# Moving the weight sums of the seven-product tiles from VectorE to GpSimd, and starting the first feed-forward with four ordinary tiles in place of five

## The chip, the core and the metric

The kernel runs on one core of a Trainium2 chip, in one launch. The metric is the device time of that launch in microseconds (us), lower is better. Four things matter on the core here: TensorE (PE in the profile: matmuls, results in PSUM), VectorE (DVE), ScalarE (ACT) and GpSimd (POOL), each with a queue of its own that runs in order, and the SP queue, which issues the loads of weights.

## What is computed

One hybrid decoder layer in float32, 512 tokens, width 1024: a SwiGLU feed-forward of width 2816, then a mixer (three groups of dilated attention with four heads each beside a gated linear recurrence, merged by sigmoid gates), then a second feed-forward; each has a norm before and after it. Cut to what matters here:

```python
def swiglu(x, w_gate, w_up, w_down):
    return (jax.nn.silu(x @ w_gate) * (x @ w_up)) @ w_down

f = swiglu(rms_norm(h, ffn1_norm_pre), ffn1_w_gate, ffn1_w_up, ffn1_w_down)
h = h + 0.5 * rms_norm(f, ffn1_norm_post)
proj = rms_norm(h, mix_norm_pre) @ w_in      # q, k, v, recurrence, gates
...
h = h + rms_norm(merged @ w_out, mix_norm_post)
f = swiglu(rms_norm(h, ffn2_norm_pre), ffn2_w_gate, ffn2_w_up, ffn2_w_down)
h = h + 0.5 * rms_norm(f, ffn2_norm_post)
```

## The kernel before

**Split numbers.** Each float32 operand of a matmul is held as two parts, hi and lo, and a product is three matmuls (hi times hi, hi times lo, lo times hi). The function `split` makes the parts: ScalarE copies the source to hi (L269), VectorE subtracts hi from the source to get lo (L270). Both operands of that subtraction lie in SBUF.

**The stream of weights.** `raw_of` loads the weights in the order in which they are used, mostly 128x2048 values at a time, from the SP queue (L215) into a tile called `raw`, of which there are two. The split parts go into `w8` tiles (four) and `w4` tiles (two). A new load waits until a `raw` tile has been read to the end, and a new split waits until TensorE has used the `w8` tile that it overwrites.

**Two kinds of tiles.** A feed-forward has 22 column tiles f of 128 columns, each with a gate and an up product. An *ordinary* tile makes both with `gemm` (L282 to L284): 2 x 8 x 3 = 48 matmuls of 512 columns. A *seven-product* tile (`seven`, L594 to L596) makes the same two results with seven products of half the size, p1 to p7: 7 x 4 x 3 = 84 matmuls of 256 columns. It needs sums of the four weight blocks u0, u1, g0, g1 and sums of blocks of the activations:

- `w_forms` makes the weight forms. Four additions of 128x512 (L570, L571, L572, L575, all VectorE) give u0+u1, u0+u1+g0 (both in the tile `s12`), u0+g0 (in place in `raw`), and u0+u1+g0+g1 (in place in `raw`). Four splits follow: a (for p1 and p2, straight from `raw`), b (from `s12`, for p6 and p5), c (from `raw`, for p7 and p4) and d (for p3). The last addition overwrites g1, so it comes after split a has read it.
- `x_forms` makes the activation forms for the first feed-forward, in five steps: `scaled`, then `first` (p1, p2, and t1), `second` (t2, p5, p7), `third` (p6, p3), `fourth` (p4). The steps need the norm's factor, so they come behind the first ordinary tile, one step behind each ordinary tile.
- The tiles t1, t2 and `s12` share two buffers (tag "s"): the first `s12` can only be written once split p5 has read t1.

**The order of the first feed-forward** (`ffn_order`, NSTD[1] = 5): ordinary tiles f = 0 to 4, then `prep` of tile 5 (its `w_forms`), then the first half of the down product of part 0 (f = 0 to 3, 48 matmuls, L388 to L390), then seven-product tiles 5 to 21, each with the `prep` of the next ahead of it and half a down product behind some of them. The second feed-forward begins with three ordinary tiles. The mixer has 16 seven-product tiles more: twelve pairs of query and key columns and four pairs of gate columns. That makes 17 + 16 + 19 = 52.

**What sets the order on an engine.** A scheduler orders each engine's instructions when the program is built, by priority and by estimated times; `high_priority` pulls weight splits (AHEAD) and reads of PSUM (EVAC) forward. On the chip each engine follows that order without exception, so an instruction that waits holds up everything behind it on its engine.

Of the kernel before, what the change touches and what calls it, by code (L numbers as in the profile page):

```python
# [19 lines left out]
KC = D // P  # L20
NF = 22
FF_PARTS = ((0, 4), (4, 8), (8, 12), (12, 16), (16, 22))
NSTD = {1: 5, 2: 3}
NG = 3
NH = 4
EPS = 1e-6
# [22 lines left out]
def ffn_order(n):  # L49

    order = [("std", f) for f in range(NSTD[n])]
    early = NSTD[n] >= FF_PARTS[0][1]
    order.append(("prep", NSTD[n]))
    if early:
        order.append(("down", 0, 0))
    for a, (f0, f1) in enumerate(FF_PARTS):
        fs = range(max(f0, NSTD[n]), f1)
        halves = () if a == 0 else (1,) if a == 1 and early else (0, 1)  # L60
        for i, f in enumerate(fs):
            if f + 1 < NF:
                order.append(("prep", f + 1))
            c, k = len(fs), len(halves)
            order.append(("prod", f, a - 1, halves[i * k // c:(i + 1) * k // c]))
    return order


def part_blocks(a):

    return (FF_PARTS[a][1] - FF_PARTS[a][0]) // 2
# [85 lines left out]
def hybrid_layer(ctx: ExitStack, tc: tile.TileContext, xT: bass.AP, xN: bass.AP, wst: bass.AP,  # L157
                 first: bass.AP, rows: bass.AP, consts: bass.AP, bias: bass.AP, out: bass.AP):
    nc = tc.nc
    DVE, ACT, PE = nc.vector, nc.scalar, nc.tensor  # L160

    cpool = ctx.enter_context(tc.tile_pool(name="cpool", bufs=1))
    bpool = ctx.enter_context(tc.tile_pool(name="bpool", bufs=6))
# [25 lines left out]
    def fb(b, sl=slice(0, D)):  # L189
        return facc[:, 2 * b:2 * b + 2, :].rearrange("p k t -> p (k t)")[:, sl]  # L190
# [16 lines left out]
    def raw_of(key):  # L207

        g, i = state["g"], state["i"]
        grp = groups[g]  # L210
        if i == 0:
            w = grp[-1][1] + grp[-1][2]
            raw = wpool.tile([P, RAW_W], F32, name="raw", tag="raw", bufs=2)
            src = bass.AP(tensor=wst.tensor, offset=wst.offset + state["off"], ap=[[w, P], [1, w]])
            nc.sync.dma_start(raw[:, :w], src)  # L215
            state["raw"] = raw
            state["off"] += w * P
        k, o, w = grp[i]
        assert k == key, (k, key)
        src = state["raw"][:, o:o + w]  # L220
        if i + 1 == len(grp):
            state["g"], state["i"] = g + 1, 0
        else:
            state["i"] = i + 1
        return src

    def fetch(key, slot=None, ahead=0):

        with tc.high_priority(offset=ahead if slot else state["ahead"]):
            src = raw_of(key)  # L230
            w = src.shape[-1]
            t = slot() if slot else w8() if w > 512 else w4()
            split(t[:, 0, :w], t[:, 1, :w], src)
            return t[:, 0, :w], t[:, 1, :w]

    def w8():
        return wpool.tile([P, 2, 1024], F32R, name="w8", tag="w8", bufs=4)

    def w4():
        return wpool.tile([P, 2, 512], F32R, name="w4", tag="w4", bufs=2)  # L240
# [27 lines left out]
    def split(dh, dl, src):  # L268
        ACT.activation(dh, src, AF.Copy)  # L269
        DVE.tensor_sub(dl, src, dh.bitcast(F32))  # L270

    def acc_ps():
        return psum.tile([P, T], F32, name="acc", tag="acc", bufs=5)

    def aux_ps():
        return psum.tile([P, T], F32, name="aux", tag="aux", bufs=3)

    def tmp(name):
        return tpool.tile([P, T], F32, name=name, tag="t")
# [104 lines left out]
    def tokens(ps, ws, x, b, fill=lambda: None):  # L384
        bl = slice(b * P, (b + 1) * P)
        for k in range(x.n):
            wh, wl = (w.rearrange("p (k c) -> p k c", k=2)[:, k % 2, :] for w in ws[k // 2])
            PE.matmul(ps, x.hi[k][:, bl], wh, start=k == 0, stop=False)  # L388
            PE.matmul(ps, x.hi[k][:, bl], wl, start=False, stop=False)  # L389
            PE.matmul(ps, x.lo[k][:, bl], wh, start=False, stop=k == x.n - 1)  # L390
            if k == x.n // 2 - 1:
                fill()
# [171 lines left out]
    def w_forms(key):  # L564

        with tc.high_priority(offset=AHEAD):
            raw = raw_of(key)
            u0, u1, g0, g1 = (raw[:, i * 512:(i + 1) * 512] for i in range(4))
            s12 = spool[0].tile([P, 2, 512], F32, name="s12", tag="s", bufs=2)
            DVE.tensor_add(s12[:, 1, :], u0, u1)  # L570
            DVE.tensor_add(s12[:, 0, :], s12[:, 1, :], g0)  # L571
            DVE.tensor_add(u0, u0, g0)  # L572
            a, b, c, d = w8(), w8(), w8(), w4()
            split(a[:, 0, :], a[:, 1, :], raw[:, 1024:2048])
            DVE.tensor_add(g1, s12[:, 0, :], g1)  # L575
            split(b[:, 0, :], b[:, 1, :], s12.rearrange("p s c -> p (s c)"))
            split(c[:, 0, :], c[:, 1, :], raw[:, 0:1024])
            split(d[:, 0, :], d[:, 1, :], g1)
            lo, hi = slice(0, 512), slice(512, 1024)
            return {"p1": a[:, :, lo], "p2": a[:, :, hi], "p6": b[:, :, lo], "p5": b[:, :, hi],  # L580
                    "p7": c[:, :, lo], "p4": c[:, :, hi], "p3": d}
# [42 lines left out]
    def ffn(n, x, r, forms_x, apool, pss):  # L624
        t, steps = forms_x
        acts = {}

        def act_at(f):

            if f // 4 not in acts:  # L630
                at = apool.tile([P, 8, T], F32R, name="act", tag="act", bufs=3)
                acts[f // 4] = Act([at[:, j, :] for j in range(4)], [at[:, 4 + j, :] for j in range(4)])
            return acts[f // 4].hi[f % 4], acts[f // 4].lo[f % 4]

        def part(a):
            f0, f1 = FF_PARTS[a]
            his, los = zip(*(act_at(f) for f in range(f0, f1)))
            return Act(his, los)

        def std_out(psg, psu, f):  # L640

            g, u = tmp("g"), tmp("u")
            if r is None:
                ACT.activation(g, psg, AF.Silu)
                DVE.tensor_mul(u, psu, g)
            else:
                DVE.tensor_mul(g, psg, r)
                ACT.activation(g, g, AF.Silu)
                DVE.tensor_mul(u, psu, r)
                DVE.tensor_mul(u, u, g)  # L650
            split(*act_at(f), u)

        def wd():
            return apool.tile([P, 2, 1024], F32R, name="wd", tag="wd", bufs=2)

        def down(a, half):
            ws = [fetch(("down", n, a, half, kk), wd, AHEAD) for kk in range(part_blocks(a))]
            for b in range(4):
                ps, y = acc_ps(), fb(b, FHALVES[half])
                tokens(ps, ws, part(a), b)  # L660
                if a == 0:
                    ACT.activation(y, ps, AF.Copy)
                else:
                    DVE.tensor_add(y, ps, y)

        def prod(f, w, a, hs_):
            g, u = tmp("g"), tmp("u")
            seven(t, w, aux_ps()[:, :HB], [g[:, h] for h in HALVES], [u[:, h] for h in HALVES])
            for half in hs_:
                down(a, half)  # L670
            ACT.activation(g, g, AF.Silu)
            DVE.scalar_tensor_tensor(u, g, -1.0, u, op0=ALU.mult, op1=ALU.mult)
            split(*act_at(f), u)

        keys = [(w, n, i) for i in range(NSTD[n]) for w in ("gate", "up")]
        forms = {}
        for ev in ffn_order(n):
            if ev[0] == "std":
                j = ev[1]
                while len(pss) < 2 * j + 2:  # L680
                    pss.append(acc_ps())
                    gemm(pss[-1], fetch(keys[len(pss) - 1]), x)
                std_out(pss[2 * j], pss[2 * j + 1], j)
                if j < len(steps):
                    steps[j]()
            elif ev[0] == "prep":
                forms[ev[1]] = w_forms(("gu", n, ev[1]))
            elif ev[0] == "down":
                down(ev[1], ev[2])
            else:  # L690
                prod(ev[1], forms.pop(ev[1]), ev[2], ev[3])
        a = len(FF_PARTS) - 1
        return lambda half, kk: ("down", n, a, half, kk), part_blocks(a), part(a)
# [28 lines left out]
    u1 = act_two(ap1)  # L722
# [20 lines left out]


    end1 = ffn(1, u1, r1, x_forms("g1a", r1, ap1), ap1, pss)
    new_h()
    for b in range(4):
# [16 lines left out]
    with ExitStack() as mx:  # L764
# [53 lines left out]
        t, steps = forms_of(um, um_t[:2], um_t[2:], apool, False)  # L818
# [171 lines left out]
    with ExitStack() as mx:  # L990
# [144 lines left out]
        for c in range(KC):  # L1135
# [16 lines left out]
                 {(1, 3): lambda: (bd2.turn(0), bd2.turn(1))})  # L1152
    keys = [(w, 2, i) for i in range(NSTD[2]) for w in ("gate", "up")]
    pss = gemm_first(keys[:NFIRST], u2, [spare(ap2)[2]],
# [127 lines left out]
```

## Time and profile before

| what | value |
|---|---|
| device time, median of 3 runs | 1244.78 us (1244.69 to 1245.48) |
| profiled execution, its own time | 1245.37 us |
| its span from the first to the last instruction | 1243.6 us |
| granted TensorE clock over the span | 0.998 |
| VectorE additions in `w_forms` | 4 x 52 |
| GpSimd instructions | 51 |

The profile is of one execution. Its time of 1245.37 us is 1.8 us more than its span (launch and end lie outside the span) and 0.6 us above the median of the three runs. A row such as `start us, us, engine line op out<-in xcount` gives when a run of equal instructions started, how long it took and which program line it comes from; a matmul's shown duration overlaps the next one's, so the pace of TensorE is read from the distance between starts.

### The profile page before, as it was taken

To read this page: it belongs to the slowest core of one execution; us is meant where nothing else is said; L and a number is where in the kernel's file an instruction comes from. 1 tells how busy PE (TensorE), PEld (TensorE's weight loads), DVE (VectorE), ACT (ScalarE), POOL (GpSimd) and SP (SyncE) were. 2 spreads that over 40 slices of the span, in tenths; PEclk is the share of its full clock that TensorE was granted. 3 is DMA by queue.
4 is the path that set the end of the run, shared out by engine and by line. 5 is a ranking of instruction groups with operands and counts; after the bars stand their busy time and mean duration, and the time that the engine had idled before them with its cause. 6 is when DMAs were issued, how large, how long until landed. Compare 5 with 4: busy or idle time off the path is not lost.

```text
span 1243.6 us, 19076 instructions
## 1 busy us (share of the span) xinstructions
PE 1232.1 (99%) x7748; PEld 1117.6 (90%) x7748; DVE 930.4 (75%) x1473; ACT 664.3 (53%) x1100; POOL 26.2 (2%) x51
## 2 busy tenths in 40 slices
PE   9999999999999999999999999999999999999997
PEld 8899999999878899999988887888899999999986
DVE  7996777796576588888575898864798667777755
ACT  7555444455355365666544788734565544445432
POOL 0000000000002000000000000000100000000000
PEclk9999999999999999999999999999999999999999
DMA  6222222235424223222243222224443222222241
GB/s 242 102 79 103 101 102 102 101 126 184 167 90 144 85 95 103 77 89 91 100 172 102 70 99 102 102 102 169 142 130 136 103 103 102 103 103 73 103 182 67
DMA packets 27383, 141.37 MB, mean 114 GB/s; under 512 B 2976, under 2 KB 6176, under 8 KB 13216
## 3 DMA queue, kind: packets, MB, share of 16 engines
q1 hardware_dynamic: 20016, 122.86, 27.9%
q0 software_dynamic: 7280, 17.30, 4.1%
q8 instruction: 60, 0.98, 0.3%
q14 instruction: 27, 0.22, 0.1%
HBM read 129.67 MB, written 6.29 MB: 109 GB/s over the span
## 4 chain that ended last, share of the span: by engine, by line
PE 89%; DVE 6%; ACT 4%; issue 1%; DVEq 0%; ACTq 0%
PE acc L594 11%; PE acc L595 11%; PE acc L596 11%; PE acc L388 7%; PE acc L389 7%; PE acc L390 7%; PE acc L282 6%; PE acc L283 6%; PE acc L284 6%; PE aux L595 3%; PE aux L594 3%; PE aux L596 3%; PE acc L793 1%; PE acc L795 1%; PE acc L794 1%
## 5 line engine op out<-in xcount | busy, mean ns | idle before, releaser
L270 DVE TENSOR_TENSOR w<-raw,w 128x1024 fp32r<-128x1024 f32 (+1 forms) x241 | 257.9, 1074 | 97.2 <-ACT w L269 64.7
L269 ACT ACTIVATE w<-raw 128x1024 fp32r<-128x1024 f32 (+1 forms) x241 | 225.2, 938 | 181.3 <-DVE raw L575 61.0
L594 PE MATMUL acc<-big,w 128*128 128x256 f32 x896 | 255.4, 285 | 0.0
L595 PE MATMUL acc<-big,w 128*128 128x256 f32 x896 | 254.4, 284 | 0.0
L596 PE MATMUL acc<-big,w 128*128 128x256 f32 x896 | 254.1, 284 | 0.0
L594 PEld LDWEIGHTS acc<-big,w 128*128 128x128 f32 x896 | 171.6, 192 | 1.0
L595 PEld LDWEIGHTS acc<-big,w 128*128 128x128 f32 x896 | 171.7, 192 | 0.6
L596 PEld LDWEIGHTS acc<-big,w 128*128 128x128 f32 x896 | 171.7, 192 | 0.0
L601 ACT ACTIVATE c<-acc 128x256 f32<-128x256 f32 x172 | 65.2, 379 | 81.4 <-PE acc L596 78.1
L389 PE MATMUL acc<-wd,act 128*128 128x512 f32 x256 | 99.8, 390 | 0.0
L388 PE MATMUL acc<-wd,act 128*128 128x512 f32 x256 | 99.6, 390 | 0.0
L390 PE MATMUL acc<-wd,act 128*128 128x512 f32 x256 | 99.4, 389 | 0.0
L594 PE MATMUL aux<-big,w 128*128 128x256 f32 x288 | 81.5, 283 | 0.0
L595 PE MATMUL aux<-big,w 128*128 128x256 f32 x288 | 81.5, 283 | 0.0
L596 PE MATMUL aux<-big,w 128*128 128x256 f32 x288 | 81.4, 283 | 0.0
L594 PE MATMUL acc<-tx,w 128*128 128x256 f32 x272 | 77.2, 284 | 0.0
L596 PE MATMUL acc<-tx,w 128*128 128x256 f32 x272 | 77.0, 283 | 0.0
L595 PE MATMUL acc<-tx,w 128*128 128x256 f32 x272 | 77.0, 283 | 0.0
L282 PE MATMUL acc<-big,w 128*128 128x512 f32 x192 | 74.7, 389 | 0.0
L283 PE MATMUL acc<-big,w 128*128 128x512 f32 x192 | 74.7, 389 | 0.0
L284 PE MATMUL acc<-big,w 128*128 128x512 f32 x192 | 74.7, 389 | 0.0
L270 DVE TENSOR_TENSOR w<-s,w 128x1024 fp32r<-128x1024 f32 x52 | 63.7, 1224 | 10.2 <-ACT w L269 10.1
(316 smaller groups left out, 2753.0 us busy)
## 6 DMA issues: line engine op xcount, KB each, us to landing
raw<-in_w SPq DMA_DIRECT2D x110, 1024.0 KB, 4.8
big<-act POOLq DMA_DIRECT2D x6, 512.0 KB, 3.4
gains<-in_rows POOLq DMA_DIRECT2D x5, 512.0 KB, 5.0
h<-in_x SPq DMA_DIRECT2D x8, 256.0 KB, 5.0
h<-in_xn POOLq DMA_DIRECT2D x4, 512.0 KB, 7.6
kept_m<-h POOLq DMA_DIRECT2D x4, 512.0 KB, 2.9
h<-kept_m POOLq DMA_DIRECT2D x4, 512.0 KB, 5.4
kept<-h POOLq DMA_DIRECT2D x4, 512.0 KB, 3.4
```

Source lines behind the costliest of these rows:

```text
L269: ACT.activation(dh, src, AF.Copy)
L270: DVE.tensor_sub(dl, src, dh.bitcast(F32))
L282: PE.matmul(ps, wh, xh, start=first, stop=False)
L283: PE.matmul(ps, wh, xl, start=False, stop=False)
L284: PE.matmul(ps, wl, xh, start=False, stop=last)
L388: PE.matmul(ps, x.hi[k][:, bl], wh, start=k == 0, stop=False)
L389: PE.matmul(ps, x.hi[k][:, bl], wl, start=False, stop=False)
L390: PE.matmul(ps, x.lo[k][:, bl], wh, start=False, stop=k == x.n - 1)
L594: PE.matmul(ps, wh, xh, start=start and k == 0, stop=False, skip_group_check=True)
L595: PE.matmul(ps, wh, xl, start=False, stop=False, skip_group_check=True)
L596: PE.matmul(ps, wl, xh, start=False, stop=k == 3, skip_group_check=True)
L601: ACT.activation(c, ps, AF.Copy)
```

## The change

Two edits. All four additions in `w_forms` go to GpSimd, in every seven-product tile. And the first feed-forward starts with four ordinary tiles (f = 0 to 3), so that tile 4 becomes a seven-product tile; behind the last ordinary tile all steps of `x_forms` that are left are issued (`third` and `fourth` together).

```diff
-NSTD = {1: 5, 2: 3}
+NSTD = {1: 4, 2: 3}
...
-    DVE, ACT, PE = nc.vector, nc.scalar, nc.tensor
+    DVE, ACT, PE, POOL = nc.vector, nc.scalar, nc.tensor, nc.gpsimd
...
             s12 = spool[0].tile([P, 2, 512], F32, name="s12", tag="s", bufs=2)
-            DVE.tensor_add(s12[:, 1, :], u0, u1)
-            DVE.tensor_add(s12[:, 0, :], s12[:, 1, :], g0)
-            DVE.tensor_add(u0, u0, g0)
+            POOL.tensor_add(s12[:, 1, :], u0, u1)
+            POOL.tensor_add(s12[:, 0, :], s12[:, 1, :], g0)
+            POOL.tensor_add(u0, u0, g0)
             a, b, c, d = w8(), w8(), w8(), w4()
             split(a[:, 0, :], a[:, 1, :], raw[:, 1024:2048])
-            DVE.tensor_add(g1, s12[:, 0, :], g1)
+            POOL.tensor_add(g1, s12[:, 0, :], g1)
...
                 std_out(pss[2 * j], pss[2 * j + 1], j)
-                if j < len(steps):
-                    steps[j]()
+                for step in steps[j:] if j == NSTD[n] - 1 else steps[j:j + 1]:
+                    step()
```

The weights of tile 4 are then streamed as one 128x2048 block (up and gate side by side), which the host's packing follows by itself.

## The prediction

> **What bounds the kernel now.** I read first the page, then the stretches of 31.09 us, then the groups by line, then the timelines around the first seven-product tile.
>
> ```profile
> span 1243.6 us, 19076 instructions
> PE 1232.1 (99%) x7748; PEld 1117.6 (90%) x7748; DVE 930.4 (75%) x1473; ACT 664.3 (53%) x1100; POOL 26.2 (2%) x51
> ...
> PE 89%; DVE 6%; ACT 4%; issue 1%; DVEq 0%; ACTq 0%
> ```
>
> TensorE is busy in 1232.1 of 1243.6 us and carries 89% of the chain that ended last. VectorE, which is relieved, carries 6%.
>
> ```profile
> 0.00:31.09 31.09, 30.04 (x132) 25.58 (x133) 23.73 (x46) 22.98 (x44) 0.20 (x4) 1.00 0.68 242
> 31.09:62.18 31.09, 31.09 (x139) 25.75 (x138) 30.94 (x38) 18.28 (x22) 0.00 (x0) 1.00 0.29 102
> ...
> 155.45:186.54 31.09, 31.09 (x218) 29.17 (x217) 23.41 (x35) 14.22 (x22) 0.00 (x0) 1.00 0.29 102
> ...
> 497.44:528.53 31.09, 31.00 (x263) 30.82 (x262) 27.10 (x56) 19.84 (x49) 0.00 (x0) 1.00 0.23 77
> ...
> 746.16:777.25 31.09, 29.70 (x130) 24.05 (x129) 24.98 (x33) 25.26 (x34) 0.00 (x0) 1.00 0.30 102
> ...
> 901.61:932.70 31.09, 31.09 (x240) 30.13 (x239) 30.33 (x38) 20.58 (x29) 1.49 (x2) 1.00 0.42 130
> ```
>
> The columns are the length, then busy time and instructions of TensorE, its weight loads, VectorE, ScalarE and GpSimd. Where TensorE idles (30.04 at the start, 29.70 in the recurrence) no weight sum is made. Where sums are made it stands still for 0 to 0.09 us in 31.09. VectorE is full in two stretches, 30.94 us in the second and 30.33 us where the second feed-forward starts: TensorE does not wait for it there, but little is in reserve.
>
> ```profile
> L594 PE MATMUL acc<-big,w 128*128 128x256 f32 x896 | 255.4, 285 | 0.0
> ...
> L282 PE MATMUL acc<-big,w 128*128 128x512 f32 x192 | 74.7, 389 | 0.0
> ```
>
> The last column, idle time ahead of the group, is zero for both kinds of matmul: TensorE runs at its own pace.
>
> **The tile that changes its kind.** The pace, from starts:
>
> ```profile
> 61.22 0.39 PE L388 MATMUL acc<-wd,act 128*128 128x512 f32 x1
> ...
> 72.10 0.28 PE L594 MATMUL acc<-big,w 128*128 128x256 f32 x1
> ...
> 82.17 0.28 PE L594 MATMUL acc<-big,w 128*128 128x256 f32 x1
> ```
>
> Between 61.22 and 72.10 lie the 48 matmuls of half a down product: 10.88 us, 0.227 each. Between 72.10 and 82.17 lie the 84 of one seven-product tile: 10.07 us, 0.120 each. Tile 4 loses 48 of the first kind and gains 84 of the second: **-0.8 us**. That is all the second edit can bring.
>
> **The additions that leave VectorE.**
>
> ```profile
> L570 DVE TENSOR_TENSOR s<-raw x52: 681/686/691, 51.4 to 1158.7; 128x512 f32<-128x512 f32 x52
> ...
> 39.82 0.68 DVE L650 TENSOR_TENSOR u<-u,g 128x512 f32<-128x512 f32 x1
> 40.42 1.22 DVE L270 TENSOR_TENSOR big<-h,big 128x1024 fp32r<-128x1024 f32 x1
> 41.55 0.68 DVE L270 TENSOR_TENSOR act<-u,act 128x512 fp32r<-128x512 f32 x1
> 42.15 1.22 DVE L480 TENSOR_TENSOR t<-h 128x1024 f32<-128x1024 f32 x1
> 43.29 2.35 DVE L270 TENSOR_TENSOR w<-raw,w 128x1024 fp32r<-128x1024 f32 x2
> ```
>
> One addition lasts 0.686 us; from start to start a 128x512 operation takes 0.60 us (39.82 to 40.42) and a 128x1024 one 1.13 us (40.42 to 41.55). So 208 additions free 208 x 0.60 = 125 us of VectorE. I cost that at **0**: the engine that sets the end does not wait for VectorE where the sums are made. At the most it is the few hundredths of a microsecond per stretch shown above, under 0.5 us in all.
>
> **What one addition takes on GpSimd.** No row shows a GpSimd addition. The ends are 0.68 us (the same operation on VectorE) and 1.22 us (VectorE on 128x1024: as many elements as GpSimd must read if it takes its two operands one after the other). I take 1.22: the only GpSimd rows here are short memsets and DMA issues, nothing that shows it at VectorE's rate. [...]
>
> **Where the path tightens: the first seven-product tile.** Tile 4 now begins one ordinary tile earlier, when VectorE is full. In the built order of the changed kernel VectorE does this from 43.29 on: both splits of the down weights and split a of tile 4 (3 x 1.13), two PSUM reads (1.20), t2 (1.13), a product (0.60), split p5 (1.13): 7.5 us, until 50.8. Only then is the buffer of t1 free, and GpSimd can begin. From there to the lo part of tile 3's result stand seven VectorE operations of 1.13 and five of 0.60, **10.9 us, all with two operands in SBUF**, and two PSUM reads (1.20). Among them are splits b, c, d of tile 4 and d of tile 5, behind all **eight** GpSimd additions of the two tiles. None can be passed: ScalarE's split b is queued ahead of its c and d splits, its Silu and tile 3's hi part, and everything on VectorE stands in line behind split b.
>
> TensorE: its ordinary tiles end at 61.22 - 10.88 = 50.34. Then come 36 down matmuls of f = 0 to 2 (8.16), 24 of p5 and p1 (2.88), 9 of p6 (1.08), and at 62.5 the 12 down matmuls that need tile 3's lo part. Before, that part had an ordinary tile's time more.
>
> When is it ready? The price depends on whether a GpSimd addition and a VectorE operation that both read two SBUF operands go on side by side.
>
> - **Taking turns**: 50.8 + 10.9 + 8 x 1.22 = 71.5; TensorE waits 9.0 us (with 0.68 per addition: 67.1, 4.6 us).
> - **Side by side**:
>
> ```profile
> 43.41 1.06 ACT L269 ACTIVATE big<-t 128x1024 fp32r<-128x1024 f32 x1 [2.10 <-DVE t L480]
> ...
> 48.98 0.61 ACT L269 ACTIVATE act<-u 128x512 fp32r<-128x512 f32 x1
> ```
>
>   two additions to 53.2, ScalarE's split b to 54.3, five VectorE splits (5.1) to 59.4, the eighth addition to 60.6, ScalarE's split d (0.61) to 61.3, four more VectorE operations (2.9) to 64.2: a wait of 1.7 us, or 0.5 us at 0.68 per addition (63.0).
>
> I take the turns, as a judgement: in these rows such pairs of reads only ever follow one another, in VectorE's queue, and nothing shows two engines at them at once. [...]
>
> A wait of that length has a second price:
>
> ```profile
> 1235.00:1243.60 8.60, 0.55 (x3) 0.12 (x1) 4.69 (x11) 1.02 (x3) 0.00 (x0) 0.70 0.32 122
> ...
> 1.05 4.63 PE L728 MATMUL aux<-ones 128*128 128x128 f32 x20 [1.05 <-DVE eps L201]
> ...
> 357.20 0.65 PE aux L448 x4
> ```
>
> In the last 8.6 us, with TensorE idle, the granted clock averages 0.70. And after the idle start 20 matmuls of 128 columns take 4.63 us, where four warm ones take 0.65 (20 would take some 2.4, allowing for the pipeline's tail). So coming back costs 0 to 2.3 us; I take 1.2.
>
> **Elsewhere.** In the first feed-forward 31.09 us hold two seven-product tiles. VectorE's 23.41 us lose 8 x 0.60 and, if it stood still through every addition, gain 8 x 1.22: 28.4, which still fits; 0. In the second feed-forward the first seven-product tile leaves VectorE as many additions less (4.8 us) as GpSimd takes turns more (9.8): 5.0 us later, about what I estimate the slack of its forms to be; 0 to 1, taken as 0. GpSimd's own DMAs stand ahead of the first additions of the mixer and of the second feed-forward:
>
> ```profile
> 382.53 2.47 POOL L815 DMA_DIRECT2D vals<-vals  x5 [2.32 <-ACT vals L803]
> ...
> 413.20 1.06 ACT L269 ACTIVATE w<-s 128x1024 fp32r<-128x1024 f32 x1 [1.31 <-PE acc L795]
> ...
> 907.15 0.74 POOL L536 DMA_DIRECT2D big<-act  x1 [2.72 <-DVE facc L549]
> ...
> 912.38 1.06 ACT L269 ACTIVATE w<-s 128x1024 fp32r<-128x1024 f32 x1 [0.37 <-PE acc L284]
> ```
>
> The last such issues end at 385.0 and 907.9; two additions later (387.4, 910.3) `s12` is full, ahead of ScalarE's split b at 413.2 and 912.4: 0. The loads on SP now wait for GpSimd's last reads of `raw` as well, which come ahead of splits c and d that they waited for already: 0.
>
> **The sum.** 1245.4 - 0.8 + 9.0 + 1.2 = 1254.8 for the profiled execution; that one stood 0.6 us above the median, so **1254.2 us**.
>
> **The rivals.**
>
> *Side by side (not slower).* GpSimd's additions don't hold VectorE. For it: TensorE has no waits elsewhere, and only the chain above costs. Against it: nothing shows such an overlap. Price: 1245.4 - 0.8 + 1.7 - 0.6 = 1245.7, or 1244.5 at 0.68. It decides if VectorE's operations between 51 and 64 us keep their 1.13 and 0.60 us from start to start. Chance 0.19.
>
> *The attention stage pays too.*
>
> ```profile
> 454.88 0.86 PE aux L872 x4
> ...
> 494.25 0.86 PE aux L872 x4
> ```
>
> One head lasts 39.4 us and holds three pairs, 12 additions; per 31.09 us that is 9.5. VectorE's 27.10 us there become 27.10 - 5.7 + 11.6 = 33.0 if all of its work had to take turns, 1.9 over. Against it: much of that work reads PSUM. From 1.02 us per addition on it decides, on that assumption; at its worst 2.4 us a head, 9.6 for four: 1263.8. Chance 0.10.
>
> *VectorE's relief shows after all.* Some wait of the start or the attention stage goes away when the order changes. To be over 0.2% it would have to remove 2.5 us, and TensorE idles less than that where sums are made. Chance 0.03.
>
> That the change doesn't do what it says is excluded: the built program has 212 additions on GpSimd, 48 matmuls of 512 columns fewer and 84 of 256 more.
>
> **How the numbers follow.** Turns at the start alone have 0.68. A measurement of this kernel can tell about 0.2%, 2.5 us, from no change. Slower by more: 0.68 + 0.10 and a little of the side-by-side case, 0.79. Within it: 0.18. Faster: 0.03. The range runs from the side-by-side case at its dearer end (1245.5) to the attention case (1263).
>
> **What would show it.** Right: VectorE operations of 128x1024 between 51 and 72 us that last about twice 1.13 or start late beside GpSimd additions; additions near 1.2 us; an idle TensorE of several microseconds ahead of L594 on `tx` (form p6) and of the down matmuls L388, near 61 to 73 us; half-speed matmuls behind it; stretches after 100 us as before. Wrong: VectorE rows unchanged beside GpSimd's, or TensorE idle in every tile.

## The result and the profile after

The changed kernel takes **1296.6 us** (median of 6 runs, 1295.79 to 1298.15), the kernel before 1245.11 us beside it: ratio 1.0414, interval 1.0401 to 1.0428. That is 51.5 us slower; 1254.2 us were predicted, with 1263.0 as the upper end. The profiled execution took 1296.45 us. From the page of the changed kernel:

```profile
span 1294.7 us, 19318 instructions
PE 1247.8 (96%) x7784; PEld 1126.0 (87%) x7784; DVE 887.0 (69%) x1269; ACT 664.7 (51%) x1106; POOL 345.8 (27%) x263
PE 63%; DVE 17%; ACT 11%; issue 4%; POOL 3%; DMA 1%; SPq 0%; DVEq 0%; ACTq 0%; POOLq 0%
```

TensorE's share of the chain fell from 89% to 63%; VectorE's rose from 6% to 17%, although it has 208 additions less to do. Its busy time fell by only 43.4 us, where the additions that left had held it for about 125 us (208 x 0.60, from start to start).

**Where the time went.** Three matmuls serve as milestones: the first L448 (a norm behind the first feed-forward), the first L282 on `big` (behind attention) and the last L388 on `wd` (near the end of the second feed-forward). The rows give minimum, median and maximum duration in ns, then the first and the last start in us. Before:

```profile
L448 PE MATMUL aux<-cst,u x64: 271/273/329, 349.1 to 901.5; 128*128 128x128 f32 x64
L282 PE MATMUL acc<-big,w x192: 389/389/389, 643.4 to 797.0; 128*128 128x512 f32 x192
L388 PE MATMUL acc<-wd,act x256: 389/389/396, 61.2 to 1202.1; 128*128 128x512 f32 x128
```

After:

```profile
L448 PE MATMUL aux<-cst,u x64: 270/273/329, 362.9 to 940.5; 128*128 128x128 f32 x64
L282 PE MATMUL acc<-big,w x192: 389/389/389, 682.4 to 836.0; 128*128 128x512 f32 x192
L388 PE MATMUL acc<-wd,act x256: 389/389/396, 50.0 to 1253.2; 128*128 128x512 f32 x128
```

The first feed-forward lost 362.9 - 349.1 = 13.8 us. Up to the end of attention the lag is 682.4 - 643.4 = 39.0, so the mixer added 25.2. The recurrence, without weight sums, added nothing (797.0 to 836.0, again 39.0). The second feed-forward brought it to 51.1, so it lost 12.1.

Stretches of the changed kernel, columns as in the prediction; the last three are the granted clock, the share of the DMA engines and GB/s:

```profile
62.18:93.27 31.09, 25.93 (x189) 24.91 (x190) 27.71 (x26) 15.53 (x25) 15.45 (x9) 0.89 0.20 68
...
155.45:186.54 31.09, 31.02 (x217) 28.96 (x216) 19.62 (x26) 14.12 (x22) 11.29 (x9) 1.00 0.29 102
...
559.62:590.71 31.09, 26.91 (x218) 25.86 (x217) 23.35 (x46) 16.24 (x45) 10.94 (x8) 1.00 0.23 77
...
963.79:994.88 31.09, 25.44 (x185) 24.94 (x185) 22.74 (x24) 14.71 (x24) 13.96 (x9) 0.89 0.18 61
```

In the steady first feed-forward (155.45) TensorE still works 31.02 of 31.09 us. The losses lie at its start (62.18), in attention (559.62) and at the start of the second (963.79). In attention VectorE is busy for only 23.35 us: it is not full there, and TensorE waits nevertheless.

**Two engines in turns.** The start, VectorE in the first fence and GpSimd in the second:

```profile
51.21 2.32 DVE L498 TENSOR_TENSOR h<-h 128x1024 f32<-128x1024 f32 x1
...
57.04 3.88 DVE L270 TENSOR_TENSOR w<-raw,w 128x1024 fp32r<-128x1024 f32 x2
60.85 2.28 DVE L270 TENSOR_TENSOR big<-h,big 128x1024 fp32r<-128x1024 f32 x1
63.05 2.29 DVE L270 TENSOR_TENSOR w<-raw,w 128x1024 fp32r<-128x1024 f32 x1
65.26 0.68 DVE L649 TENSOR_TENSOR u<-acc,r 128x512 f32<-128x512 f32 x1
...
70.09 0.68 DVE L270 TENSOR_TENSOR act<-u,act 128x512 fp32r<-128x512 f32 x1
```

```profile
52.52 2.15 POOL L571 TENSOR_TENSOR s<-s,raw 128x512 f32<-128x512 f32 x1
...
58.25 2.13 POOL L570 TENSOR_TENSOR s<-raw 128x512 f32<-128x512 f32 x1
60.45 1.59 POOL L571 TENSOR_TENSOR s<-s,raw 128x512 f32<-128x512 f32 x1
```

Operations of 1.22 us on VectorE show 2.28 to 2.32, and GpSimd's additions 1.59 to 2.15, where the shortest of the run takes 1.26: I read each as its own time and a wait for the other. The minimum, and the means of the four lines:

```profile
L575 POOL TENSOR_TENSOR raw<-s,raw x53: 1263/1290/2293, 55.9 to 1223.8; 128x512 f32<-128x512 f32 x53
```

```profile
L571 POOL TENSOR_TENSOR s<-s,raw 128x512 f32<-128x512 f32 x53 | 91.9, 1733 | 4.0
L572 POOL TENSOR_TENSOR raw<-raw 128x512 f32<-128x512 f32 x53 | 84.2, 1589 | 0.0
L570 POOL TENSOR_TENSOR s<-raw 128x512 f32<-128x512 f32 x53 | 77.2, 1457 | 252.1 <-DMA raw<-in_w 186.8 <-DVE big L270 63.9 <-issue 1.2
L575 POOL TENSOR_TENSOR raw<-s,raw 128x512 f32<-128x512 f32 x53 | 69.8, 1318 | 250.6 <-DVE w L270 242.4 <-DVE xch L912 8.2
```

VectorE's read of PSUM (L649) keeps 0.68. TensorE meanwhile:

```profile
59.00 0.28 PE L595 MATMUL aux<-big,w 128*128 128x256 f32 x1
65.99 0.58 PE L594 MATMUL acc<-big,w 128*128 128x256 f32 x1 [6.71 <-DVE u L649]
...
68.72 0.37 PE L596 MATMUL aux<-big,w 128*128 128x256 f32 x1
```

It waits 6.71 us for L649, which stands behind two such turns. Then twelve matmuls take 68.72 - 65.99 = 2.73 us instead of 12 x 0.120 = 1.44: half speed behind this gap, at a granted clock of 0.50 from 65.99 to 68.80.

**Attention**, VectorE, GpSimd, ScalarE and TensorE in the same few microseconds:

```profile
487.00 1.65 DVE L950 TENSOR_TENSOR facc<-facc,e 128x512 f32<-128x512 f32 x1
...
490.26 1.29 DVE L953 TENSOR_SCALAR facc<-facc,w 128x128 f32<-128x128 f32 x1
```

```profile
486.41 1.68 POOL L575 TENSOR_TENSOR raw<-s,raw 128x512 f32<-128x512 f32 x1 [8.17 <-DVE xch L912]
```

```profile
488.13 0.63 ACT L269 ACTIVATE w<-raw 128x512 fp32r<-128x512 f32 x1 [1.68 <-POOL raw L575]
```

```profile
488.79 0.63 PE L941 MATMUL aux<-cst,facc 128*128 128x128 f32 x4 [0.56 <-ACT w L269]
...
491.69 0.30 PE L941 MATMUL aux<-cst,facc 128*128 128x128 f32 x1 [1.92 <-DVE facc L953]
```

The fourth addition, held up by VectorE, stands ahead of ScalarE's split d. The profile puts the first wait of TensorE's transposes L941 (0.56 us) down to that split, which ended at 488.76; their input, made by VectorE's L950 in 1.65 us beside the same addition, was ready only 0.11 us earlier, so the record doesn't separate the two. The next transposes wait for VectorE's L953, which took 1.29 us beside GpSimd's addition. L953 by group, before:

```profile
L953 DVE TENSOR_SCALAR facc<-facc,w 128x256 f32<-128x256 f32 x12 | 3.5, 351 | 0.0
L953 DVE TENSOR_SCALAR facc<-facc,w 128x128 f32<-128x128 f32 x4 | 1.1, 283 | 0.0
```

After:

```profile
L953 DVE TENSOR_SCALAR facc<-facc,w 128x128 f32<-128x128 f32 x4 | 5.2, 1289 | 0.0
```

Between 440 and 640 us TensorE's waits add up to 17.6 us: 8.1 for L953, 4.9 for the small exchange step at the end of a head (L912, L919), 4.0 for ScalarE's copies out of PSUM (L601) and 0.6 for split d. The rest of the mixer's 25.2 us stands in no wait that the profile shows.

**The second feed-forward's start** waits through ScalarE's queue, twice:

```profile
968.79 0.39 PE L594 MATMUL acc<-tx,w 128*128 128x256 f32 x1 [3.34 <-ACT c L601]
...
975.62 0.39 PE L594 MATMUL acc<-big,w 128*128 128x256 f32 x1 [2.31 <-ACT c L601]
```

```profile
964.89 1.06 ACT L269 ACTIVATE big<-ts 128x1024 fp32r<-128x1024 f32 x1 [4.76 <-DVE ts L553]
...
973.72 0.63 ACT L269 ACTIVATE w<-raw 128x512 fp32r<-128x512 f32 x1 [4.98 <-POOL raw L575]
```

ScalarE's copies L601, which free PSUM for TensorE, stand behind a split of activation forms (waiting for VectorE) and behind split d (waiting for GpSimd's fourth addition).

### The profile page after: what moved, and what is told of

Same layout as the page of the kernel before. It is cut to its first block, busy times and chain, and to the rows that moved or that the text cites. A ratio compares the mean times of both kernels' runs of the same rounds, so it can differ in the third digit from the quotient of the medians.

```text
span 1294.7 us, 19318 instructions
## 1 busy us (share of the span) xinstructions
PE 1247.8 (96%) x7784; PEld 1126.0 (87%) x7784; DVE 887.0 (69%) x1269; ACT 664.7 (51%) x1106; POOL 345.8 (27%) x263
## 3 DMA queue, kind: packets, MB, share of 16 engines
q1 hardware_dynamic: 20016, 122.86, 26.8%
## 4 chain that ended last, share of the span: by engine, by line
PE 63%; DVE 17%; ACT 11%; issue 4%; POOL 3%; DMA 1%; SPq 0%; DVEq 0%; ACTq 0%; POOLq 0%
PE acc L594 7%; DVE w L270 7%; PE acc L595 7%; PE acc L596 7%; PE acc L388 7%; PE acc L389 7%; PE acc L390 7%; ACT w L269 5%; PE acc L282 4%; PE acc L283 4%; PE acc L284 4%; POOL raw L575 3%; PE aux L596 1%; PE aux L595 1%; PE aux L594 1%
## 5 line engine op out<-in xcount | busy, mean ns | idle before, releaser
L270 DVE TENSOR_TENSOR w<-raw,w 128x1024 fp32r<-128x1024 f32 (+1 forms) x242 | 287.7, 1192 | 174.4 <-ACT w L269 125.0
L594 PE MATMUL acc<-big,w 128*128 128x256 f32 x912 | 261.8, 287 | 13.7 <-DVE u L649 6.7
L595 PE MATMUL acc<-big,w 128*128 128x256 f32 x912 | 259.4, 284 | 0.0
L596 PE MATMUL acc<-big,w 128*128 128x256 f32 x912 | 259.4, 285 | 0.0
L594 PEld LDWEIGHTS acc<-big,w 128*128 128x128 f32 x912 | 175.8, 193 | 18.5 <-ACT c L601 10.7
L595 PEld LDWEIGHTS acc<-big,w 128*128 128x128 f32 x912 | 176.0, 193 | 0.6
L596 PEld LDWEIGHTS acc<-big,w 128*128 128x128 f32 x912 | 176.0, 193 | 0.0
L570 POOL TENSOR_TENSOR s<-raw 128x512 f32<-128x512 f32 x53 | 77.2, 1457 | 252.1 <-DMA raw<-in_w 186.8
L575 POOL TENSOR_TENSOR raw<-s,raw 128x512 f32<-128x512 f32 x53 | 69.8, 1318 | 250.6 <-DVE w L270 242.4
L601 ACT ACTIVATE c<-acc 128x256 f32<-128x256 f32 x175 | 65.9, 377 | 71.1 <-PE acc L596 67.2
L388 PE MATMUL acc<-wd,act 128*128 128x512 f32 x256 | 99.8, 390 | 0.0
L571 POOL TENSOR_TENSOR s<-s,raw 128x512 f32<-128x512 f32 x53 | 91.9, 1733 | 4.0
L594 PE MATMUL acc<-tx,w 128*128 128x256 f32 x276 | 80.0, 290 | 7.9 <-ACT c L601 7.7
L270 DVE TENSOR_TENSOR w<-s,w 128x1024 fp32r<-128x1024 f32 x53 | 76.8, 1449 | 11.9 <-ACT w L269 11.8
L594 PE MATMUL aux<-big,w 128*128 128x256 f32 x296 | 84.4, 285 | 0.0
L595 PE MATMUL aux<-big,w 128*128 128x256 f32 x296 | 84.3, 285 | 0.0
L596 PE MATMUL aux<-big,w 128*128 128x256 f32 x296 | 84.3, 285 | 0.0
L572 POOL TENSOR_TENSOR raw<-raw 128x512 f32<-128x512 f32 x53 | 84.2, 1589 | 0.0
L596 PE MATMUL acc<-tx,w 128*128 128x256 f32 x276 | 78.9, 286 | 0.0
```

Source lines behind the costliest of these rows:

```text
L570: POOL.tensor_add(s12[:, 1, :], u0, u1)
L571: POOL.tensor_add(s12[:, 0, :], s12[:, 1, :], g0)
L572: POOL.tensor_add(u0, u0, g0)
L575: POOL.tensor_add(g1, s12[:, 0, :], g1)
L594: PE.matmul(ps, wh, xh, start=start and k == 0, stop=False, skip_group_check=True)
L595: PE.matmul(ps, wh, xl, start=False, stop=False, skip_group_check=True)
```

## The experiments

The theory that this profile suggests: GpSimd's reads from SBUF and VectorE's reads from SBUF exclude each other, and every chain that passes through both engines becomes longer. Rivals: the longer chain by GpSimd's own slowness, another order on the engines, the lost ordinary tile. The loss by stage (milestones as above, against 349.1, 643.4 and 1202.1 us), for all kernels:

| kernel | us, median | ratio to before, interval | first FF | mixer | second FF |
|---|---|---|---|---|---|
| changed kernel | 1296.6 | 1.0414 [1.0401, 1.0428] | +13.8 | +25.2 | +12.1 |
| e1: GpSimd, five ordinary tiles | 1294.7 | 1.0403 [1.0377, 1.0429] | +12.5 | +24.8 | +12.4 |
| e2: VectorE, four ordinary tiles | 1252.23 | 1.0054 [1.0039, 1.0069] | +7.0 | +0.1 | -0.1 |
| e3: before, idle GpSimd reads beside | 1331.61 | 1.0692 [1.0675, 1.0710] | +21.9 | +35.4 | +27.6 |
| e4: two fills for each addition | 1244.1 | 0.9988 [0.9978, 0.9997] | -1.1 | -0.1 | -0.1 |
| e5: GpSimd in the feed-forwards only | 1272.4 | 1.0215 [1.0199, 1.0230] | +15.5 | -0.1 | +12.6 |
| e6: GpSimd in the mixer only | 1269.06 | 1.0194 [1.0179, 1.0209] | -0.4 | +23.5 | -0.1 |
| e7: fourth addition on VectorE | 1280.75 | 1.0289 [1.0256, 1.0322] | +13.9 | +14.2 | +7.7 |
| e8: three fills for each addition | 1247.95 | 1.0019 [1.0009, 1.0028] | -0.5 | +3.2 | 0.0 |
| e9: one copy for each addition | 1252.56 | 1.0059 [1.0043, 1.0075] | +4.3 | +3.5 | +0.4 |
| e10: e2, two tiles read out early | 1244.93 | 0.9996 [0.9987, 1.0006] | -0.8 | -0.1 | +0.6 |
| e11: e2, four tiles read out early | 1244.95 | 0.9998 [0.9989, 1.0006] | -1.1 | -0.1 | -0.1 |
| e12: changed kernel, read out early | 1297.24 | 1.0418 [1.0399, 1.0436] | +13.1 | +25.7 | +12.8 |

**e1 and e2, each edit alone.** e1 is the changed kernel with five ordinary tiles, e2 the changed kernel with all four sums on VectorE.

```diff
-NSTD = {1: 4, 2: 3}
+NSTD = {1: 5, 2: 3}
```

> The changed kernel with five ordinary tiles again: the GpSimd edit alone. Theory (GpSimd and VectorE take turns at SBUF reads, and the tile swap takes away the time that hid it at the start): the wait at the first seven-product tile goes, the rest stays: 1296.6 less some 12 us of lost TensorE time at the start, plus 0.8 for the tile: about 1285 (1282 to 1289). Rival (the fewer ordinary tiles cost nothing, all of the loss is in the sums): 1297.4.

The fifth ordinary tile gives back next to nothing: 1294.7 us, where 1282 to 1289 were expected. The start keeps its wait in another place, at the down product that needs the last tile's result:

```profile
67.27 0.80 PE L388 MATMUL acc<-wd,act 128*128 128x512 f32 x1 [4.56 <-ACT act L269]
```

```diff
-            POOL.tensor_add(s12[:, 1, :], u0, u1)
+            DVE.tensor_add(s12[:, 1, :], u0, u1)
...
```

> The kernel before with four ordinary tiles and the new order of the steps, sums on VectorE: the other edit alone. Theory: VectorE is full there; from 50.8 us on it has 10.9 + 1.2 us and eight additions of 0.60, to 67.7, against 62.5 for TensorE: a wait of about 5 us, perhaps 2 more for the clock, less 0.8: 1249 to 1252. Rival (only GpSimd costs anything): 1244.3.

The swap alone costs 7 us, all at the start. Its wait, on TensorE and then on VectorE:

```profile
63.24 0.79 PE L388 MATMUL acc<-wd,act 128*128 128x512 f32 x1 [4.43 <-DVE g L647]
```

```profile
61.90 0.68 DVE L575 TENSOR_TENSOR raw<-s,raw 128x512 f32<-128x512 f32 x1
62.50 0.68 DVE L647 TENSOR_TENSOR g<-acc,r 128x512 f32<-128x512 f32 x1
```

The read of the last ordinary tile stands behind the second seven-product tile's additions. The swap makes none of the loss elsewhere; the additions on GpSimd make all of it without the swap (e1: 24.8 and 12.4 us).

**e3, reads and nothing else.** The kernel before, with four additions on GpSimd per tile that read `s12` into a buffer nobody reads:

```diff
             DVE.tensor_add(u0, u0, g0)
+            for i in range(4):
+                POOL.tensor_add(acc, s12[:, 1, :], s12[:, 0, :])
```

> The kernel before, sums on VectorE in its own order, and beside each tile's sums four GpSimd additions of the same size that read the s12 tile and write a dead tile that nobody reads: contention without any path through GpSimd. Theory (turns are the cause): VectorE's two-operand operations stretch to about twice their time and the kernel is slower by a good part of the 51 us: 1260 to 1285. Rival A (the cost is the slow additions on the path) and rival B (the cost is the order that the scheduler made): no change, 1244 to 1247.

It costs more than the theory said, 86 us. Nobody uses the results and VectorE kept its own additions, but its splits became longer still (1483 ns mean, against 1222 before and 1315 in the changed kernel). The reuse of `s12` waits for these reads as well, but VectorE was held up by that only once, for 3.9 us. One GpSimd addition took 6.22 us beside VectorE's queue:

```profile
L270 DVE TENSOR_TENSOR w<-raw,w 128x1024 fp32r<-128x1024 f32 x174 | 257.3, 1483 | 72.8 <-ACT w L269 46.3 <-PE acc L598 26.0
L574 POOL TENSOR_TENSOR acc<-s 128x512 f32<-128x512 f32 x208 | 368.1, 1770 | 483.0 <-DVE s L571 427.8 <-DVE st L921 42.7
```

```profile
55.62 6.22 POOL L574 TENSOR_TENSOR acc<-s 128x512 f32<-128x512 f32 x1 [55.17 <-DVE s L571]
```

**e4 and e8, the same places without reads.** Each addition becomes two (e4) or three (e8) fills of its output:

```diff
-            POOL.tensor_add(u0, u0, g0)
+            POOL.memset(u0, 0.5)
+            POOL.memset(u0, 0.5)
```

> The changed kernel with each GpSimd addition replaced by two fills of the same 128x512 tile, which write the same places behind the same waits for those who read them before, but read nothing (the weight forms hold a constant: the sums are left out). Theory: without GpSimd reads VectorE keeps 0.60 and 1.13 us from start to start, and what is left is the chain at the start, 1 to 3 us: 1245 to 1250. Rivals A and B (slow path, or the order): still 1275 to 1297.

> The changed kernel, with each GpSimd sum replaced by three fills of the same output with a constant, about 1.58 us together by the 0.525 us of one fill measured before: as long as the sums took beside VectorE (mean 1.52), and without a read from SBUF. The sums are left out. Theory (VectorE is slowed by GpSimd's reads, and GpSimd's time by itself is nearly harmless): 1244 to 1249. Rival, that the lengthened chain of four sums on GpSimd, as long as it became, is what made ScalarE and TensorE wait: 1260 to 1290.

With two fills (1.05 us together) the loss is gone (1244.1 us, a little below the range expected), and VectorE's splits take 1222 ns again. With three, GpSimd is busy for as long as in the changed kernel and TensorE loses 3.2 us in the mixer. The page of e8, and its split group:

```profile
PE 1233.6 (99%) x7784; PEld 1117.9 (90%) x7784; DVE 821.0 (66%) x1269; ACT 665.6 (53%) x1106; POOL 342.0 (27%) x687
```

```profile
L270 DVE TENSOR_TENSOR w<-raw,w 128x1024 fp32r<-128x1024 f32 x174 | 212.0, 1222 | 117.6 <-ACT w L269 69.3 <-PE acc L604 47.5
```

GpSimd is busy for 342.0 us here and 345.8 in the changed kernel; VectorE, with the same 1269 instructions, for 821.0 and 887.0. The longer fills cost 1247.95 - 1244.1 = 3.9 us, so the length of GpSimd's chain by itself is worth at most about that (the longer fills also slow VectorE's `tensor_scalar`, as the last section shows), and the rest of the 51.5 goes with the reads.

**e9, half the reading.** Each addition becomes a copy of one block:

```diff
-            POOL.tensor_add(u0, u0, g0)
+            POOL.tensor_copy(u0, g0)
```

> The changed kernel, with each GpSimd sum replaced by a copy of one 128x512 block into the same output: one block is read from SBUF where the sum reads two. The sums are left out (weight forms hold copies). Theory (GpSimd's reading is what VectorE's two-operand operations take turns with): VectorE's rows stay above the 1.22 us they take alone, and the loss is between none and the whole, about half for half the reading: some 1262 to 1275. Rival, that only GpSimd operations with two inputs contend: like the fills, 1244 to 1249, and VectorE's rows at 1.22.

VectorE's splits are lengthened (1250 and 1295 ns in this trace for 1222 and 1224 before), so one operand is enough to contend. The cost, 7.4 us, is far less than half: the expectation in proportion to the reading missed. A copy takes about half as long as an addition (637 ns mean for 1318 on L575):

```profile
L270 DVE TENSOR_TENSOR w<-s,w 128x1024 fp32r<-128x1024 f32 x53 | 68.7, 1295 | 16.9 <-ACT w L269 16.9
L575 POOL COPY raw<-s 128x512 f32<-128x512 f32 x53 | 33.8, 637 | 341.1 <-DVE w L270 330.0 <-DVE xch L912 10.6
```

**e5 and e6, one stage at a time.** e5 as shown; e6 has "pair" in place of "gu", and five ordinary tiles.

```diff
+            ADD = POOL if key[0] == "gu" else DVE
-            POOL.tensor_add(s12[:, 1, :], u0, u1)
+            ADD.tensor_add(s12[:, 1, :], u0, u1)
...
```

> The changed kernel, with the sums on GpSimd in the two feed-forwards only; the sums of the mixer's pair tiles, which run in the attention stage, stay on VectorE as before. Four ordinary tiles lead the first feed-forward. Theory (GpSimd's reads from SBUF slow VectorE's two-operand operations beside them, and each stage pays by what it has queued on VectorE): the attention stage goes back to TensorE's pace, the feed-forwards' losses stay: 1245.1 + 12.4 (start of the first feed-forward) + 9.5 (start of the second) + 3 (steady tiles) - 0.8 (an ordinary tile fewer) = about 1269. Rival, that the attention stage was late only because the feed-forward ahead of it left its work late: about 1294.

> The kernel before (five ordinary tiles, feed-forward sums on VectorE), with the sums of the mixer's pair tiles alone on GpSimd, which run in the attention stage. Theory (each stage pays for its own overlap of GpSimd and VectorE): 1245.1 + 24 = about 1269, and the losses of this run and of its complement add up to those of the changed kernel. Rival, that the losses came from the feed-forwards and were only carried on: 1245 to 1247.

Both came out near the 1269 us expected (1272.4 and 1269.06), and the losses add up: 26.8 + 23.5 = 50.3 of 51.5 us. Each stage pays for its own overlap; nothing is carried on.

**e7, the addition on which ScalarE's split waits.**

```diff
-            POOL.tensor_add(g1, s12[:, 0, :], g1)
+            DVE.tensor_add(g1, s12[:, 0, :], g1)
```

> The changed kernel, with the fourth sum of each tile (g1 = s12 + g1, on whose result ScalarE's split waits at the head of its queue) back on VectorE; three of four sums stay on GpSimd. Theory of contention alone: a quarter less GpSimd time and 52 additions more on VectorE, the loss falls by about a quarter, to some 1283. Rival, that most of the loss comes through ScalarE's queue behind the fourth sum: the attention stage's 24 us and part of the second start go, about 1262 to 1268.

The loss falls by 32% (22 to 38% by the interval; the four runs spread from 1277.62 to 1286.64), which holds the 25% of contention alone and not the rival's 1262 to 1268. The mixer gains 11.0 us and the second start 4.4, so ScalarE's queue behind the fourth addition does count, but the first start gains nothing and more than half of the mixer's loss stays.

**e10, e11 and e12, the read of PSUM moved forward.** e11 (from e2) and e12 (from the changed kernel) as shown; e10 (from e2) with the condition `n == 1 and j >= 2`.

```diff
-                std_out(pss[2 * j], pss[2 * j + 1], j)
+                with tc.high_priority(offset=EVAC if n == 1 else 0):
+                    std_out(pss[2 * j], pss[2 * j + 1], j)
```

> The sums on VectorE and four ordinary tiles, as in the run that took 1252.23, with the results of the first feed-forward's last two ordinary tiles (third and fourth) taken out of PSUM at the priority that the seven-product tiles' copies have. Theory (with four tiles on VectorE, the only loss is TensorE's wait of 4.6 us and less behind the fourth tile's copy, which stood on VectorE after the second tile's sums): the wait goes, and the swap of one tile shows its 0.8 us: 1244 to 1246. Rival, that VectorE is simply short of time at that start, so that whatever goes first makes something else late: 1249 to 1253.

> As the run before, with all four ordinary tiles of the first feed-forward taken out of PSUM at that priority. Theory: 1244 to 1246 as well. Rival, VectorE short of time at the start: 1249 to 1253.

> The changed kernel (all sums on GpSimd, four ordinary tiles), with the results of the first feed-forward's four ordinary tiles taken out of PSUM at the priority that the seven-product tiles' copies have, as in the run on VectorE that took 1244.95. Theory (at the start too the price is the turns that GpSimd's additions take, and VectorE has no time left there): part of the 12.4 us of the start goes, since TensorE no longer waits behind the fourth tile's second read of PSUM, but the forms p6 and those of the second tile stay late: 1288 to 1293, with some 5 to 9 us left between 31 and 124 us. Rival (the start was lost by the place of that read alone): 1283 to 1285, nothing left there.

On VectorE the swap's loss was the place of that read alone: with it moved, 1244.93 and 1244.95 us. On GpSimd the same edit gains nothing: 1297.24 us, above the range expected and above the rival's. The wait moves on to the matmuls of p6:

```profile
71.63 0.58 PE L594 MATMUL acc<-tx,w 128*128 128x256 f32 x1 [6.14 <-ACT c L601]
```

What came last there is not the form p6, whose lo part was ready at 69.0, but ScalarE's copy L601 of 71.20 to 71.58, which has to take p1's result out of PSUM before p6 is added to it. It stands behind split d, which waited for GpSimd's fourth addition, the link seen in the second feed-forward:

```profile
68.05 2.11 POOL L575 TENSOR_TENSOR raw<-s,raw 128x512 f32<-128x512 f32 x1 [1.23 <-DVE w L270]
```

```profile
70.19 0.63 ACT L269 ACTIVATE w<-raw 128x512 fp32r<-128x512 f32 x1 [2.93 <-POOL raw L575]
```

No version beats the kernel before by more than the measurement can tell; e10 and e11 equal it. And e4, where the sums are left out and the fills cost nothing that shows, gains only 1.5 us: so little was there to be won.

## Why the prediction was right or wrong

**Bound, pace, relief: right.** TensorE sets the time of the kernel before; VectorE's relief was worth next to nothing (e4 gains 1.5 us in all, about 0.8 of it from the tile). The tile's -0.8 us agrees with e10 (-0.8) and e11 (-1.1) at the first milestone, though e6, with five ordinary tiles and VectorE's sums up to there, shows -0.4, so the trace can hardly tell it from scatter.

**One GpSimd addition: 1.22 taken, 1.26 at shortest, 1.52 mean** (323.1 us over 212). The upper bound from VectorE's 128x1024 row was near.

**Taking turns: right, and shown.** The lo part of tile 3 was forecast for 71.5; its row starts at 70.09 and ends at 70.77. That it came so near is in part luck: the sum counted a full turn for each of eight additions, 9.8 us, where VectorE's rows are stretched by 5.5 us in all, it idles 1.7 for ScalarE, and the two PSUM reads that the sum left out take 1.2. What was wrong is the place of the wait. TensorE stopped after its matmul of 59.00, at a PSUM buffer that L649 still had to read, before it reached the down matmuls. The step "at 62.5 the 12 down matmuls" assumed that all ahead of them was ready. e12 shows that the loss didn't depend on it: move that read, and the matmuls of p6 wait for ScalarE's copy instead. The start was forecast at 9.0 + 1.2 - 0.8 = 9.4 us; the first feed-forward lost 13.8. Its waits between 30 and 125 us add up to 9.7 us (6.7 for L649, 3.0 for copies L601), near the 9.0. The half-speed price was 2.73 - 1.44 = 1.3 us for the 1.2 taken (the middle of 0 to 2.3, so near by luck), and it was paid once: the granted clock is 1.00 from 68.90 to 363 us. What the sum left out are short stops behind the start: from 70 us to the first L448 TensorE's starts lie 7.3 us further apart in all than at 0.120 and 0.227 each, mostly ahead of L594, in stops of up to 1.4 us, of which 3.4 us show as waits for L601.

Reads make the difference here: beside additions VectorE's 128x1024 rows took 2.28 us for 1.22, beside GpSimd's fills, which only write, 1.222 mean (e8). L953, a `tensor_scalar`, took 1.29 us mean on 128x128 in the changed kernel, against 0.28 before.

**The step that failed: no loss behind the start.** The sum had nothing for the second feed-forward and for attention, and there lie 12.1 + 25.2 = 37.3 of the 51.1 us. "Elsewhere" took the second feed-forward at "0 to 1, taken as 0" because 5.0 us later was "about what I estimate the slack of its forms to be"; it lost 12.1. The slack was estimated, not followed through the queues: VectorE's forms and split d both stand ahead of ScalarE's copies out of PSUM, and TensorE waits for those.

**The attention rival: right in kind, wrong in its premise.** It asked whether VectorE's work still fits (33.0 us in 31.09 at the worst) and gave at most 9.6 us. VectorE does fit, with 23.35 us busy, and the stage loses 25.2. By the 16 matmuls L872 of the four heads, one head lasts (606.3 - 471.2) / 3 = 45.0 us, against (573.5 - 454.7) / 3 = 39.6 before: 5.4 a head for the 2.4 allowed. Before, and after:

```profile
L872 PE MATMUL aux<-qk x16: 379/379/379, 454.7 to 573.5; 128*128 128x256 f32 x16
```

```profile
L872 PE MATMUL aux<-qk x16: 379/379/379, 471.2 to 606.3; 128*128 128x256 f32 x16
```

The term that was mis-sized is a latency: the exchange, weights, products and transposes at the end of a head alternate between VectorE, ScalarE and TensorE, so a turn lost there can be lost to TensorE, full engine or not: 13.0 us of waits there are for L953 and the exchange. The reason given against it, that much of that work reads PSUM, passed over L950 and L953, which read SBUF.

**Side by side, and relief that shows: excluded**, by the rows of 2.28 us and by e4. The ends of the range, 1245.5 and 1263, don't quite follow from the prices worked out above them (1245.7 and 1263.8); nothing hangs on that.

## What to carry to other kernels

Before moving element-wise work to GpSimd, ask what it reads and what VectorE reads at that time: here, where GpSimd read SBUF while VectorE's operations read two operands there, they took turns (2.28 us for 1.22), and the move gave VectorE back in latency a good part of what it took off its load (66.0 us of busy time, 887.0 against 821.0 in e8). Whether busy times still add up to less than the stage decides only where nobody waits for a single result (in attention VectorE was busy for 23.35 of 31.09 us, and the mixer lost 25.2); in stages that alternate between engines, follow each result to the matmul that needs it. And an engine that works for an in-order queue puts its delays on everything that stands behind in that queue (here ScalarE's split d waited 4.98 us for GpSimd's addition, and TensorE 2.31 us for a copy behind that split).

## What the runs showed of the hardware that I had not expected

- The turns weren't fair: a GpSimd addition, 1.26 us at its shortest, took up to 6.22 beside VectorE's queue (e3). The longest VectorE split in the changed kernel took 2.32 us, no more than its own time and one addition. One addition at the start of e12:

```profile
52.42 3.41 POOL L570 TENSOR_TENSOR s<-raw 128x512 f32<-128x512 f32 x1 [51.97 <-DVE big L270]
```

- Fills leave VectorE's two-operand splits alone (1222 ns mean before and in e8), but not `tensor_scalar`: 128x256 took 351 ns mean before and 695 beside three fills (e8):

```profile
L961 DVE TENSOR_SCALAR facc<-facc,w 128x256 f32<-128x256 f32 x12 | 7.7, 695 | 0.0
```

- A gap on TensorE can cost more than itself. In the second feed-forward's first waits it idled 3.34 and 2.31 us, and the granted clock was 0.50 from 970.03 to 973.44 and from 976.86 to 980.27. Behind the 1.28 us that it idled before 86.93 the clock stayed at 1.00.
